# Laying SBUF out anew at fixed residues of 256 bytes in a hybrid decoder block (pooling mixer, gated linear attention, SwiGLU)

## The chip, the core and the metric

The kernel runs on one core of one Trainium2 chip. What counts is the device time of one execution in microseconds (us). Three runs of the kernel before took 1494.24, 1494.49 and 1495.74 us; their median is 1494.49 us. Where a figure below belongs to the profiled execution, that is one further run, of 1494.63 us.

## The reference, cut to what matters

The input is a block of 256 tokens by 2048 channels in float32. It goes through one decoder layer:

```
h = rms_norm(x);  z = h @ w_in                     # 2048 x 11280, split into p, q, k, v, g_lr, r, gate_logits
y_a = pool_mixer(p) @ w_branch_a                   # trailing means over windows of 2, 4, 8, 16 tokens
o   = gated linear attention(q, k, v, log_sigmoid(g_lr @ w_gate_up + b_gate) / 16)
y_b = (rms_norm(o) * silu(r)) @ w_branch_b
mixed = (sigmoid(g0) * y_a + sigmoid(g1) * y_b) @ w_out
x = x + rms_norm(mixed)
h = rms_norm(x)
x = x + rms_norm((silu(h @ w_ffn_gate) * (h @ w_ffn_up)) @ w_ffn_down)   # d_ff 5632
```

Nearly all the arithmetic is in the products with the weight matrices, 285 MB of float32 that come from HBM once.

## The kernel before, in words

**Precision.** TensorE multiplies float32r, a shortened float32. So each weight and each activation is split into a high part (a copy rounded to float32r) and a low part (the rest), and each product of the reference is three products on TensorE: weight high times activation high, weight low times activation high, weight high times activation low. These are the three `pe.matmul` lines that stand in a row everywhere: L337 to L339, L348 to L350, L408 to L410.

**Jobs and units.** The function `plan` lists jobs; a job makes 512 output columns for all 256 tokens (two row tiles `t`). A job is made of units, and each unit has one slot of split weights, `wh` and `wl`:

- A `Step` takes 256 rows of the weight matrix (two k-tiles): one DMA into `raw`, ScalarE copies it to `wh` (L317), VectorE subtracts to `wl` (L321). With weights as the moving operand it is twelve matmuls of 512 columns (L348 to L350), called wide below. Where the job is `across` (kinds p, q, k), the activations are the moving operand and the weights the stationary one: twenty-four matmuls of 256 columns (L337 to L339).
- A `Part` belongs to the 46 fast jobs. These do the first eight of their k-tiles by Strassen's scheme with seven products instead of eight, on two tiles of `blocks`: twelve matmuls of 256 columns each (L408 to L410), called narrow below. The seven are q1, q2 and q4, which use activations as they are, and r5, q6, q7 and r3, which use sums of activations (the list `COMBOS`). These sums have tiles of their own, made by `combine` and placed by `extra`: `x`, `ox` or `fx`.

A fast job with 16 k-tiles has four wide units and runs its units in the order of `merged`: q2, wide, q4, the next job's q1, r3, the next job's r5, wide, the next job's q6, wide, the next job's q7, wide. Jobs that follow each other keep this going without a gap.

**What sets the order.** The order is a list that the kernel builds at the start (`units`, `order`), walked by the loop at its end. `prepare_to` runs `BUFS` = 4 units ahead of the multiplications. SyncE's queue starts the weight DMAs, ScalarE and VectorE split, TensorE multiplies, and GpSimd starts a few accumulating DMAs and does small powers.

**Memory.** A tile pool places its tiles one behind the other, so where a tile starts depends on the sizes of what stands ahead of it. Weight slots come from pool `wp`, and a slot is as large as the widest unit needs, 4224 bytes per partition (16.5 times 256). Activations come from `one`: class `Act` makes, for each group of four k-tiles, a tile for the high parts and a tile for the low parts, 4096 bytes each. All of it stays in place, and tiles with the same tag share a place in turn.

**Starting residues.** A matmul reads two operands: the moving one streams through the array, the stationary one (128 columns of four bytes, 512 bytes per partition) is loaded ahead of it. What matters below is where an operand starts, modulo 256 bytes. In the built program of the kernel before these are:

| operand | before | after |
|---|---|---|
| weight slots `wh`, `wl` | 96 and 224, by turns | 64 |
| activations h (first norm), m, f, high and low | 0 | 0 |
| activations y, o, h2: groups 0 and 1 | 32 | 0 |
| activations o, h2: groups 2 and 3 | 160 | 0 |
| sums `x` | 160 | 128 |
| sums `ox` | 32 and 160 | 0 |
| sums `fx` | 224 | 128 |
| `blocks`, scratch | 224 | 64 |

Here y is the pooled branch, o the attention output, m the mixed branches, f the FFN's inner activations, h2 the second normed input.

Of the kernel before, what the change touches and what calls it, by code (L numbers as in the profile page):

```python
# [8 lines left out]
F32 = mybir.dt.float32  # L9
# [5 lines left out]
P = 128  # L15
# [17 lines left out]
BLOCKS = 3  # L33
AHEAD = 12
# [66 lines left out]
def tile_hybrid_block(ctx: ExitStack, tc: tile.TileContext, *aps):  # L101
# [6 lines left out]
    one = ctx.enter_context(tc.tile_pool(name="one", bufs=1))  # L108
    wp = ctx.enter_context(tc.tile_pool(name="wp", bufs=BUFS))
    scr = ctx.enter_context(tc.tile_pool(name="scr", bufs=SCRS))  # L110
    st = ctx.enter_context(tc.tile_pool(name="st", bufs=4))
# [6 lines left out]
    late = {}  # L118

# [18 lines left out]

    xa = [one.tile([P, D], F32, tag=f"X{t}", name=f"x{t}") for t in range(NT)]
    ident = one.tile([P, P], F32, tag="ident", name="ident")  # L140
    masks = two_st.tile([P, 64 * MASKED + P], I32, tag="masks", name="masks")
    counts = two_st.tile([P, 16], F32, tag="counts", name="counts")
    rows = [one.tile([n, P], F32, tag=f"rows{n}", name=f"rows{n}") for n in (16, 68)]
# [11 lines left out]
    first = st.tile([P, 4], F32, tag="first", name="first")  # L155
# [26 lines left out]
    def rstd_of(ss, n, width, tag):  # L182
        m = st.tile([P, width], F32, tag="ms", name=nm("ms"))
        dve.tensor_scalar(m, ss, 1.0 / n, EPS, op0=ALU.mult, op1=ALU.add)
        r = one.tile([P, width], F32, tag=tag, name=nm(tag))
        pool.tensor_tensor(r, m, mhalf[:, :width], op=ALU.pow)
        return r

    def extra(a):


        if a.name == "o":
            k = [two_st.tile([P, 2, 4, P], F32R, tag=f"K{i}", name=nm("ox")) for i in range(2)]
            q = [[two_st.tile([P, 4, P], F32R, tag=f"{x}{i}", name=nm("ox")) for i in range(2)] for x in ("Q", "AD")]
            return [tuple(x) for x in q] + [(x[:, 0], x[:, 1]) for x in k]
        if a.name[0] == "f":
            if not late:
                early.close()
                late["pool"] = ctx.enter_context(tc.tile_pool(name="late", bufs=1, reuse_waits="tile"))
            x = [late["pool"].tile([P, len(COMBOS), 4, P], F32R, tag=f"fx{i}", name=nm("fx")) for i in range(2)]  # L200
        else:
            x = [one.tile([P, len(COMBOS), 4, P], F32R, tag=f"R{i}", name=nm("x")) for i in range(2)]
        return [(x[0][:, n], x[1][:, n]) for n in range(len(COMBOS))]

    class Act:


        def __init__(self, name, groups, tag):
            self.name = name
            self.hi = [one.tile([P, 4, T], F32R, tag=f"{tag}{g}h", name=f"{name}{g}h") for g in range(groups)]  # L210
            self.lo = [one.tile([P, 4, T], F32R, tag=f"{tag}{g}l", name=f"{name}{g}l") for g in range(groups)]
# [85 lines left out]
    class Step:  # L297
# [16 lines left out]
        def high(self):  # L314
            self.load()
            self.hi = wp.tile([P, GK, self.j.width], F32R, tag="wh", name=nm("wh"))
            act.activation(self.hi, self.raw, AF.Copy)  # L317

        def low(self):
            self.lo = wp.tile([P, GK, self.j.width], F32R, tag="wl", name=nm("wl"))  # L320
            dve.tensor_tensor(self.lo, self.raw, f32(self.hi), op=ALU.subtract)  # L321
# [32 lines left out]
    class Part:  # L354
# [27 lines left out]
        def high(self):  # L382
            self.hi = wp.tile([P, 4, HW], F32R, tag="wh", name=nm("wh"))
            act.activation(self.hi, self.src, AF.Copy)  # L384

        def low(self):
            self.lo = wp.tile([P, 4, HW], F32R, tag="wl", name=nm("wl"))
            dve.tensor_tensor(self.lo, self.src, f32(self.hi), op=ALU.subtract)  # L388
# [69 lines left out]
    def total(part, ts, tag):  # L458

        w = len(ts)  # L460
        ss = st.tile([P, w], F32, tag="ss", name=nm("ss"))
        dve.tensor_reduce(ss, part[:, ts[0]:ts[0] + w, :], axis=mybir.AxisListType.X, op=ALU.add)
        return rstd_of(ss, D, w, tag)
# [71 lines left out]
    def r_done(n):  # L535
        def done(j, ts):
            glow = two_st.tile([P, NT, RANK], F32, tag="glow", name="glow") if n == 0 else None
# [29 lines left out]
    def gates_low(glow):  # L567
# [9 lines left out]
        gl["P"] = [one.tile([P, 4, T], F32, tag=f"B{2 + p}h", name=f"P{p}") for p in range(2)]  # L577
        gl["S"] = [one.tile([P, 4, T], F32, tag=f"B{2 + p}l", name=f"S{p}") for p in range(2)]
# [125 lines left out]
    def gla_out(h, t, v, silu):  # L704
# [7 lines left out]
        ss = st.tile([P, 1], F32, tag="sso", name=nm("sso"))  # L712
        act.activation(scratch(), ps, AF.Square, accum_out=ss)
        m = st.tile([P, 1], F32, tag="mso", name=nm("mso"))
        r = st.tile([P, 1], F32, tag="rso", name=nm("rso"))
# [23 lines left out]
    def chunk(tiles, t, n, tag, name):  # L739
        if not tiles:  # L740
            tiles += [one.tile([P, D], F32, tag=f"{tag}{a}", name=f"{name}{a}") for a in range(NT)]
        return tiles[t][:, n * CW:(n + 1) * CW]
# [68 lines left out]
    def out_done(n):  # L811
        def done(j, ts):
# [3 lines left out]
            for t in ts:  # L816
                if mg[t] is None:
                    mg[t] = one.tile([P, D], F32, tag=f"Y{t}", name=f"mg{t}")
# [66 lines left out]
    def down_done(part, n):  # L885
        def done(j, ts):
# [3 lines left out]
            for t in ts:  # L890
                if ff[t] is None:
                    ff[t] = one.tile([P, D], F32, tag=f"Y{t}", name=f"ff{t}")
# [8 lines left out]
            if part == 2 and n == 2:  # L901

                ss = st.tile([P, NT], F32, tag="ss", name=nm("ss"))
# [8 lines left out]
    def finish(t):  # L912
        m = st.tile([P, 1], F32, tag="ms", name=nm("ms"))
# [166 lines left out]
```

## Time and profile before

| quantity | value |
|---|---|
| median of three runs | 1494.49 us |
| the profiled execution | 1494.63 us |
| its span, first to last instruction | 1492.8 us |
| outside the span | 1.83 us |
| PE busy | 1475.1 us, 9156 matmuls |
| DVE busy | 1221.7 us |
| ACT busy | 907.7 us |
| POOL busy | 73.0 us |
| read from HBM | 284.84 MB, 194 GB/s over the span |

PE is TensorE's matrix side and PEld its loading of stationary operands, DVE is VectorE, ACT is ScalarE, POOL is GpSimd. L408 is line 408 of the kernel before. Matmuls overlap in the record: one of 256 columns is shown as 0.28 us long while the next one starts about 0.12 us after it. So what a matmul costs is read from the distance between starts, and the simplest way is to take a unit of twelve and read how long it is from its first start to the first start of what follows. A view by stretches does this: each row has the stretch, its length, the busy time of PE in it with the number of matmuls that touch it (a few more than start in it, because the neighbours overlap the edges), the granted clock and the load of the DMA engines.

### The profile page before, as it was taken

How to read it: one execution, taken by the hardware profiler on the slowest of the kernel's cores; microseconds unless marked ns; L12 is line 12 of the kernel's file. 1: busy time of each engine (PE TensorE's matmuls, PEld its weight loads, DVE VectorE, ACT ScalarE, POOL GpSimd, SP SyncE). 2: the span in 40 equal slices, each digit the busy share in tenths (PEclk: the TensorE clock that was granted, in tenths of full speed). 3: DMA queues.
4: the chain of work that ended last, by engine and by line, in shares of the span. 5: the costliest groups of instructions: out<-in, count | busy, mean ns of one | idle time of the engine just before them, and what ended most of it. 6: DMA issues, size and time to landing. Idle time of an engine off the chain costs nothing.

```text
span 1492.8 us, 23506 instructions
## 1 busy us (share of the span) xinstructions
PE 1475.1 (99%) x9156; PEld 1311.3 (88%) x9156; DVE 1221.7 (82%) x1359; ACT 907.7 (61%) x1185; POOL 73.0 (5%) x96
## 2 busy tenths in 40 slices
PE   8999999999999999999999999999999999999997
PEld 8988999888888888888878889898898888988886
DVE  6755445788899887799778899887889898888997
ACT  6457433556666665556566666666666665666663
POOL 2000000000100000000000000000000000000001
PEclk9999999999999999999999999999999999999999
DMA  8857665335668578659855677667766777676654
GB/s 286 272 173 226 215 192 176 124 111 175 228 206 248 190 241 268 201 155 295 247 173 168 215 220 231 214 220 228 236 212 213 225 226 218 224 235 222 204 180 141
DMA packets 88896, 314.70 MB, mean 211 GB/s; under 512 B 10140, under 2 KB 10352, under 8 KB 88528
## 3 DMA queue, kind: packets, MB, share of 16 engines
q1 hardware_dynamic: 77616, 279.15, 55.5%
q0 software_dynamic: 8160, 28.59, 10.0%
q10 hardware_dynamic: 3008, 5.45, 1.0%
q8 instruction: 72, 1.18, 0.3%
q14 instruction: 40, 0.33, 0.1%
HBM read 284.84 MB, written 4.19 MB: 194 GB/s over the span
## 4 chain that ended last, share of the span: by engine, by line
PE 88%; DVE 4%; issue 3%; DMA 2%; ACT 1%; POOL 0%; SPq 0%; DVEq 0%; ACTq 0%; POOLq 0%
PE acc L348 16%; PE acc L349 16%; PE acc L350 16%; PE ac L409 6%; PE ac L408 6%; PE ac L410 5%; PE acc L410 4%; PE acc L408 4%; PE acc L409 4%; PE acc L339 3%; PE acc L338 3%; PE acc L337 3%; PE tr L663 1%; DVE wl L321 1%; PE tr L180 1%
## 5 line engine op out<-in xcount | busy, mean ns | idle before, releaser
L317 ACT ACTIVATE wh<-raw 128x1024 fp32r<-128x1024 f32 (+1 forms) x336 | 355.3, 1059 | 316.9 <-PE acc L350 144.9
L321 DVE TENSOR_TENSOR wl<-raw,wh 128x1024 fp32r<-128x1024 f32 (+1 forms) x336 | 410.7, 1223 | 140.6 <-ACT wh L317 138.8
L388 DVE TENSOR_TENSOR wl<-blocks,wh 128x1024 fp32r<-128x1024 f32 x322 | 391.2, 1222 | 77.6 <-ACT wh L384 73.2
L384 ACT ACTIVATE wh<-blocks 128x1024 fp32r<-128x1024 f32 x322 | 338.1, 1058 | 157.0 <-PE acc L350 65.7
L408 PE MATMUL ac<-wh,x 128*128 128x256 f32 x396 | 111.1, 280 | 0.0
L410 PE MATMUL ac<-wh,x 128*128 128x256 f32 x396 | 110.9, 280 | 0.0
L409 PE MATMUL ac<-wl,x 128*128 128x256 f32 x396 | 110.9, 280 | 0.0
L380 POOL DMA_DIRECT2D blocks<-blocks x46 | 39.8, 865 | 822.0 <-DVE wl L321 365.9
L408 PEld LDWEIGHTS ac<-wh,x 128*128 128x128 f32 x396 | 74.4, 188 | 3.1
L409 PEld LDWEIGHTS ac<-wl,x 128*128 128x128 f32 x396 | 74.3, 188 | 2.9
L410 PEld LDWEIGHTS ac<-wh,x 128*128 128x128 f32 x396 | 74.8, 189 | 0.0
L348 PE MATMUL acc<-wh,h22h 128*128 128x512 f32 x176 | 70.1, 398 | 0.1
L349 PE MATMUL acc<-wl,h22h 128*128 128x512 f32 x176 | 69.4, 394 | 0.0
L350 PE MATMUL acc<-wh,h23l 128*128 128x512 f32 x176 | 69.3, 394 | 0.0
L348 PE MATMUL acc<-wh,h23h 128*128 128x512 f32 x176 | 69.2, 394 | 0.0
L350 PE MATMUL acc<-wh,h22l 128*128 128x512 f32 x176 | 69.2, 394 | 0.0
L349 PE MATMUL acc<-wl,h23h 128*128 128x512 f32 x176 | 69.2, 393 | 0.0
L373 DVE TENSOR_TENSOR blocks<-blocks,blocks 128x1024 f32<-128x1024 f32 x46 | 56.3, 1224 | 1.3
L369 DVE TENSOR_TENSOR blocks<-blocks,blocks 128x1024 f32<-128x1024 f32 x46 | 56.2, 1221 | 0.7
L371 DVE TENSOR_TENSOR blocks<-blocks 128x1024 f32<-128x1024 f32 x46 | 56.1, 1219 | 0.1
L348 PE MATMUL acc<-wh,h3h 128*128 128x512 f32 (+1 forms) x128 | 50.0, 391 | 0.0
L349 PE MATMUL acc<-wl,h3h 128*128 128x512 f32 (+1 forms) x128 | 49.9, 390 | 0.0
(538 smaller groups left out, 4112.7 us busy)
## 6 DMA issues: line engine op xcount, KB each, us to landing
raw<-in_w_in_dram SPq DMA_DIRECT2D x128, 512.0 KB, 4.1
raw<-in_w_ffn_gate_dram SPq DMA_DIRECT2D x48, 512.0 KB, 4.3
raw<-in_w_ffn_up_dram SPq DMA_DIRECT2D x48, 512.0 KB, 4.4
blocks<-blocks POOLq DMA_DIRECT2D x46, 512.0 KB, 6.1
blocks<-in_w_ffn_down_dram SPq DMA_DIRECT2D x44, 512.0 KB, 4.3
raw<-in_w_ffn_down_dram SPq DMA_DIRECT2D x44, 512.0 KB, 4.4
blocks<-in_w_in_dram SPq DMA_DIRECT2D x40, 512.0 KB, 4.4
blocks<-in_w_ffn_gate_dram SPq DMA_DIRECT2D x40, 512.0 KB, 4.3
```

The source lines that it names most:

```text
L317: act.activation(self.hi, self.raw, AF.Copy)
L321: dve.tensor_tensor(self.lo, self.raw, f32(self.hi), op=ALU.subtract)
L348: pe.matmul(ps, ah, hi[:, i, cs], start=first, stop=False, skip_group_check=j.fast)
L349: pe.matmul(ps, ah, lo[:, i, cs], start=False, stop=False, skip_group_check=j.fast)
L350: pe.matmul(ps, al, hi[:, i, cs], start=False, stop=last, skip_group_check=j.fast)
L369: dve.tensor_tensor(b12, b12, b22, op=ALU.add)
L373: dve.tensor_tensor(b21, b21, b12, op=ALU.add)
L384: act.activation(self.hi, self.src, AF.Copy)
L388: dve.tensor_tensor(self.lo, self.src, f32(self.hi), op=ALU.subtract)
L408: pe.matmul(dst, ah, wh, start=i == 0 and p in ("q1", "r5"), stop=False, skip_group_check=True)
L409: pe.matmul(dst, ah, wl, start=False, stop=False, skip_group_check=True)
L410: pe.matmul(dst, al, wh, start=False, stop=i == 3 and p in EARLY, skip_group_check=True)
```

## The change

Nothing of the arithmetic changes, and the order of instructions is the same on every engine. New pools stand at the start of SBUF: `his` for the high parts of activations, `los` for the low parts, `rest` for the tiles that hold Y and one of the two tiles of sums, and `st`, which moves up between them. Padding tiles of 64 and 192 bytes shift the pools `his` and `wp`. A helper `placed` takes a tile of a fixed size (4352 bytes for a weight slot, 17 times 256; 8448 bytes for a tile of sums, 33 times 256) and returns a view that starts some bytes into it. The residues that come out of it are the right column of the table above.

By the built programs, the distance D from the start of a matmul's moving operand to the start of the stationary operand that is loaded for the next matmul, modulo 256, changes as follows (counts of matmuls of 512 and of 256 columns; 192 matmuls of 264 columns and the small ones are left out, and a few single ones at other distances too):

| D | 0 | 32 | 64 | 96 | 128 | 160 | 192 | 224 |
|---|---|---|---|---|---|---|---|---|
| wide, before | 27 | 836 | 799 | 0 | 9 | 857 | 831 | 0 |
| wide, after | 14 | 0 | 125 | 0 | 0 | 0 | 3220 | 0 |
| narrow, before | 223 | 467 | 1177 | 571 | 305 | 437 | 1264 | 572 |
| narrow, after | 17 | 0 | 3158 | 0 | 6 | 0 | 1834 | 1 |

The narrow row holds the matmuls of 256 columns of the `across` jobs too (1152 of them; before, most of D = 96 and 224; after, D = 64). Beside this, small things move: the two staging tiles for the norm vectors (`rows`) are taken from the scratch buffers instead of places of their own, some small tiles in `st` get 2 buffers instead of 4 (`ms`, `sso`, `mso`, `rso`), `ss` and `first` go to `one`, and `glow` is allocated at the start. The built programs have the same waits on PE, DVE and SP apart from the first microseconds, where a few waits for scratch buffers on ACT fall on neighbouring instructions, and POOL has a wait on its own earlier work ahead of the powers for `rso`.

```
+LINE = 256
+PAD_A, PAD_B, PAD_W = 64, 0, 192
+ROOM_W = 4352
+AT_X, AT_F = 128, 64
+ROOM_X = 8448
...
     one = ctx.enter_context(tc.tile_pool(name="one", bufs=1))
+    his, st, los, rest = [ctx.enter_context(tc.tile_pool(name=n, bufs=b))
+                          for n, b in (("his", 1), ("st", 4), ("los", 1), ("rest", 1))]
     wp = ctx.enter_context(tc.tile_pool(name="wp", bufs=BUFS))
     scr = ctx.enter_context(tc.tile_pool(name="scr", bufs=SCRS))
-    st = ctx.enter_context(tc.tile_pool(name="st", bufs=4))
...
+    def placed(pool, shape, tag, name, lead=0, room=0):
+
+        n = 1
+        for k in shape:
+            n *= k
+        t = pool.tile([P, max(room // 4, n)], F32R, tag=tag, name=name)[:, lead // 4:lead // 4 + n]
+        if len(shape) == 2:
+            return t.rearrange("p (a b) -> p a b", a=shape[0])
+        return t.rearrange("p (a b c) -> p a b c", a=shape[0], b=shape[1])
...
+    for p_, n in ((his, PAD_A), (los, PAD_B), (wp, PAD_W)):
+        if n:
+            p_.tile([P, n // 4], F32, tag="pad", name=nm("pad"), bufs=1)
...
-    rows = [one.tile([n, P], F32, tag=f"rows{n}", name=f"rows{n}") for n in (16, 68)]
+    rows = [scratch()[:n, :P] for n in (16, 68)]
...
-        m = st.tile([P, width], F32, tag="ms", name=nm("ms"))
+        m = st.tile([P, width], F32, tag="ms", name=nm("ms"), bufs=2)
...
-            x = [late["pool"].tile([P, len(COMBOS), 4, P], F32R, tag=f"fx{i}", name=nm("fx")) for i in range(2)]
+            x = [placed(late["pool"], (len(COMBOS), 4, P), f"fx{i}", nm("fx"), AT_F, ROOM_X) for i in range(2)]
         else:
-            x = [one.tile([P, len(COMBOS), 4, P], F32R, tag=f"R{i}", name=nm("x")) for i in range(2)]
+            x = [placed(pool_, (len(COMBOS), 4, P), f"R{i}", nm("x"), AT_X, ROOM_X) for i, pool_ in enumerate((his, rest))]
...
-            self.hi = [one.tile([P, 4, T], F32R, tag=f"{tag}{g}h", name=f"{name}{g}h") for g in range(groups)]
-            self.lo = [one.tile([P, 4, T], F32R, tag=f"{tag}{g}l", name=f"{name}{g}l") for g in range(groups)]
+            self.hi = [placed(his, (4, T), f"{tag}{g}h", f"{name}{g}h") for g in range(groups)]
+            self.lo = [placed(los, (4, T), f"{tag}{g}l", f"{name}{g}l") for g in range(groups)]
...
-            self.hi = wp.tile([P, GK, self.j.width], F32R, tag="wh", name=nm("wh"))
+            self.hi = placed(wp, (GK, self.j.width), "wh", nm("wh"), room=ROOM_W)
...
-            self.lo = wp.tile([P, GK, self.j.width], F32R, tag="wl", name=nm("wl"))
+            self.lo = placed(wp, (GK, self.j.width), "wl", nm("wl"), room=ROOM_W)
...
-            self.hi = wp.tile([P, 4, HW], F32R, tag="wh", name=nm("wh"))
+            self.hi = placed(wp, (4, HW), "wh", nm("wh"), room=ROOM_W)
...
-            self.lo = wp.tile([P, 4, HW], F32R, tag="wl", name=nm("wl"))
+            self.lo = placed(wp, (4, HW), "wl", nm("wl"), room=ROOM_W)
...
-        ss = st.tile([P, 1], F32, tag="sso", name=nm("sso"))
+        ss = st.tile([P, 1], F32, tag="sso", name=nm("sso"), bufs=2)
...
-            tiles += [one.tile([P, D], F32, tag=f"{tag}{a}", name=f"{name}{a}") for a in range(NT)]
+            tiles += [(rest if tag == "Y" else one).tile([P, D], F32, tag=f"{tag}{a}", name=f"{name}{a}")
+                      for a in range(NT)]
```

More of the change, by code (lines that the diff above doesn't have):

```diff
@@ L141, in tile_hybrid_block @@
     masks = two_st.tile([P, 64 * MASKED + P], I32, tag="masks", name="masks")
+    glow = two_st.tile([P, NT, RANK], F32, tag="glow", name="glow")
     counts = two_st.tile([P, 16], F32, tag="counts", name="counts")
-    rows = [one.tile([n, P], F32, tag=f"rows{n}", name=f"rows{n}") for n in (16, 68)]
+    rows = [scratch()[:n, :P] for n in (16, 68)]
     cols = one.tile([P, 84], F32, tag="cols", name="cols")
@@ L153, in tile_hybrid_block @@
     pool.memset(mhalf, -0.5)
-    first = st.tile([P, 4], F32, tag="first", name="first")
+    first = one.tile([P, 4], F32, tag="first", name="first")
     act.activation(first, mhalf, AF.Copy)
@@ L460, in total @@
         w = len(ts)
-        ss = st.tile([P, w], F32, tag="ss", name=nm("ss"))
+        ss = one.tile([P, w], F32, tag="ss", name=nm("ss"), bufs=2)
         dve.tensor_reduce(ss, part[:, ts[0]:ts[0] + w, :], axis=mybir.AxisListType.X, op=ALU.add)
@@ L536, in done @@
         def done(j, ts):
-            glow = two_st.tile([P, NT, RANK], F32, tag="glow", name="glow") if n == 0 else None
             for t in range(NT):
@@ L576, in gates_low @@
         dve.tensor_tensor(gT[64:64 + RANK], g, f32(gT[:RANK]), op=ALU.subtract)
-        gl["P"] = [one.tile([P, 4, T], F32, tag=f"B{2 + p}h", name=f"P{p}") for p in range(2)]
-        gl["S"] = [one.tile([P, 4, T], F32, tag=f"B{2 + p}l", name=f"S{p}") for p in range(2)]
+        gl["P"] = [f32(placed(his, (4, T), f"B{2 + p}h", f"P{p}")) for p in range(2)]
+        gl["S"] = [f32(placed(los, (4, T), f"B{2 + p}l", f"S{p}")) for p in range(2)]
         for p in range(2):
@@ L711, in gla_out @@
             pe.matmul(ps, lo[:, s, :], v[:, tj, 0], start=False, stop=n == len(terms) - 1)
-        ss = st.tile([P, 1], F32, tag="sso", name=nm("sso"))
+        ss = st.tile([P, 1], F32, tag="sso", name=nm("sso"), bufs=2)
         act.activation(scratch(), ps, AF.Square, accum_out=ss)
-        m = st.tile([P, 1], F32, tag="mso", name=nm("mso"))
-        r = st.tile([P, 1], F32, tag="rso", name=nm("rso"))
+        m = st.tile([P, 1], F32, tag="mso", name=nm("mso"), bufs=2)
+        r = st.tile([P, 1], F32, tag="rso", name=nm("rso"), bufs=2)
         dve.tensor_scalar(m, ss, 1.0 / DV, EPS, op0=ALU.mult, op1=ALU.add)
@@ L817, in done @@
                 if mg[t] is None:
-                    mg[t] = one.tile([P, D], F32, tag=f"Y{t}", name=f"mg{t}")
+                    mg[t] = rest.tile([P, D], F32, tag=f"Y{t}", name=f"mg{t}")
                     xr[t] = one.tile([P, D], F32, tag=f"X{t}", name=f"xr{t}")
@@ L891, in done @@
                 if ff[t] is None:
-                    ff[t] = one.tile([P, D], F32, tag=f"Y{t}", name=f"ff{t}")
+                    ff[t] = rest.tile([P, D], F32, tag=f"Y{t}", name=f"ff{t}")
                 if part == 0:
@@ L901, in done @@
             if part == 2 and n == 2:
-                ss = st.tile([P, NT], F32, tag="ss", name=nm("ss"))
+                ss = one.tile([P, NT], F32, tag="ss", name=nm("ss"), bufs=2)
                 dve.tensor_reduce(ss, part3[:, :, :3], axis=mybir.AxisListType.X, op=ALU.add)
@@ L912, in finish @@
     def finish(t):
-        m = st.tile([P, 1], F32, tag="ms", name=nm("ms"))
+        m = st.tile([P, 1], F32, tag="ms", name=nm("ms"), bufs=2)
         dve.tensor_scalar(m, part3[:, t, 3:], 1.0 / D, rs["3"][:, t:t + 1], op0=ALU.mult, op1=ALU.add)
```

## The prediction

> **What bounds the kernel now.** I read the page first, then who TensorE waits for, then single stretches of TensorE's work. The page's head, its engines, the granted clock and the chain that ended last:
>
> ```profile
> span 1492.8 us, 23506 instructions
> PE 1475.1 (99%) x9156; PEld 1311.3 (88%) x9156; DVE 1221.7 (82%) x1359; ACT 907.7 (61%) x1185; POOL 73.0 (5%) x96
> PEclk9999999999999999999999999999999999999999
> PE 88%; DVE 4%; issue 3%; DMA 2%; ACT 1%; POOL 0%; SPq 0%; DVEq 0%; ACTq 0%; POOLq 0%
> ```
>
> TensorE (PE) is busy for 99% of the span at the full clock, and the chain runs through it. Its longest waits, in total, times and longest:
>
> ```profile
> PE tr L180 <- DMA x<-in_x_dram: 1.4, 3, 0.8
> PE tr L152 <- DVE scr L149: 1.1, 1, 1.1
> PE acc L337 <- ACT h3h L219: 1.0, 1, 1.0
> PE acc L349 <- DVE wl L321: 0.9, 2, 0.7
> ```
>
> The largest is 1.4 us, all for x at the start. So the kernel is as long as 3,360 wide and 5,016 narrow matmuls one behind the other (counted in the built program), and only what changes the distance from one start to the next can change the time. The change does not touch the number or order of matmuls. The question is whether that distance depends on where the operands lie. Stretches of TensorE, one unit each (columns: stretch, length, PE busy with the matmuls touched, clock, load of the DMA engines, GB/s); all are twelve matmuls from first start to first start, save rows three and four, which are twenty-four:
>
> ```profile
> 145.58:148.38 2.80, 2.80 (x13) 1.00 0.78 265
> 148.38:151.19 2.81, 2.81 (x14) 1.00 0.53 185
> 215.82:218.62 2.80, 2.80 (x27) 1.00 0.58 187
> 218.62:221.44 2.82, 2.82 (x27) 1.00 0.63 192
> 370.18:371.56 1.38, 1.38 (x13) 1.00 0.81 315
> 796.29:799.04 2.75, 2.75 (x13) 1.00 0.76 219
> 801.85:804.60 2.75, 2.75 (x14) 1.00 0.55 179
> 804.60:807.39 2.79, 2.79 (x14) 1.00 0.56 185
> 807.39:808.80 1.41, 1.41 (x13) 1.00 0.02 6
> 812.97:815.73 2.76, 2.76 (x15) 1.00 0.16 56
> 815.73:817.14 1.41, 1.41 (x14) 1.00 0.82 279
> 821.31:824.08 2.77, 2.77 (x14) 1.00 0.63 200
> 824.08:825.45 1.37, 1.37 (x14) 1.00 1.02 404
> 847.45:850.24 2.79, 2.79 (x14) 1.00 0.46 185
> 850.24:851.61 1.37, 1.37 (x14) 1.00 0.35 24
> 851.61:853.02 1.41, 1.41 (x14) 1.00 0.74 290
> 970.60:972.04 1.44, 1.44 (x14) 1.00 0.68 253
> 1404.96:1406.33 1.37, 1.37 (x14) 1.00 0.14 57
> ```
>
> In every row PE is busy throughout, so nothing was waited for, and the clock is 1.00. Yet equal work takes 2.75 to 2.81 us when wide and 1.37 to 1.44 us when narrow. The DMA load does not sort them: 1.37 us stands beside 1.02 and 0.14, 1.41 us beside 0.02 and 0.82. The distance D between a matmul's moving operand and the next matmul's stationary one does. It matters because both are read at once, as the loads show:
>
> ```profile
> 821.31 0.40 PE L348 MATMUL acc<-wh,h23h 128*128 128x512 f32 x1
> ...
> 821.32 0.19 PEld L349 LDWEIGHTS acc<-wl,h23h 128*128 128x128 f32 x1
> 821.55 0.19 PEld L350 LDWEIGHTS acc<-wh,h23l 128*128 128x128 f32 x1
> ```
>
> The load for L349 starts 0.01 us after the matmul of L348. With D from the built program, the wide rows are 2.80 us at D = 160 (145.58), 2.81 at 32 (148.38), 2.79 at 64 (804.60, 847.45) and 2.75 to 2.77 at 192 (796.29, 801.85, 812.97, 821.31). The narrow rows are 1.44 us at D = 0 (970.60). At D = 64 and 192 there are two lengths: at 64 1.38 (370.18), 1.37 (850.24, 1404.96) and 1.41 (815.73), at 192 1.37 (824.08) and 1.41 (807.39, 851.61). Which of the two comes depends on what ran before. Behind a wide unit of the same D it is the short one (824.08 behind 821.31 at 192; 850.24 behind 847.45 at 64). Behind a wide unit of the other D it is the long one (807.39 behind 804.60; 815.73 behind 812.97). 851.61, at 192 behind a narrow unit at 64, is long too. I take this to be two streams of reads that meet in the same part of SBUF and fall into a fixed rhythm.
>
> **The change part by part.** It removes and adds no work; each term is a number of units times a difference of two rows.
>
> Wide units. There are 3360/12 = 280. At D = 192 stand 831/12 = 69 now and 3220/12 = 268 after. The 199 that get there win 2.80 (the middle of 2.79 to 2.81) less 2.76 (the middle of 2.75 to 2.77), 0.04 us each: −8.0 us. Bounds: 0.02 us, from 2.79 and 2.77, gives −4.0; 0.06, from 2.81 and 2.75, gives −11.9.
>
> Narrow units without sums (q1, q2, q4, and the few that use `ox`): 1834/12 = 153, all at D = 192 after. By `merged`, q2 and q4 each stand right behind a wide unit at D = 192, which is the pattern of 824.08, so I take 1.37. q1 stands behind q4 with the same residues on both sides, so nothing changes between them, and I take 1.37 too; no row shows such a pair, since slots alternate today, and if q1 were at 1.41, 46 units would lose 0.04 us, 1.8 us. Before, 51 units last 1.385 us or less; the first of these is 370.18, the last 1404.96. So 102 more are short: 102 × (1.41 − 1.37) = −4.1 us.
>
> Narrow units with sums (r3, r5, q6, q7): 2015/12 = 168, at D = 64 after. q6 and q7 follow a wide unit at D = 192 (815.73: 1.41), r3 follows a narrow one at the other D (851.61: 1.41), r5 follows r3. I take 1.41 for all. All these 168 could also be short, −6.7 us; this goes into a rival.
>
> Narrow units at poor distances: 965 matmuls, 80 units, stand at D = 0, 128 or 160 now. Priced by 970.60 at D = 0, they go from 1.44 to 1.41 before anything else: 80 × 0.03 = −2.4 us. Those at 128 and 160 may be nearer 1.41, then it is −0.6 for D = 0 alone.
>
> `across` units: 1143 matmuls, 95 twelves. Now they take 2.80 and 2.82 us by turns for twenty-four, 1.405 for twelve. After, D = 64 throughout with 1.37 or 1.41 to choose from. No unit leads into it from a wide one of the same D, so I take 1.41: +0.5 us; the bounds are +0.5 and −3.3.
>
> The small edits cost nothing in my sum. Extra waits at the start fall on ACT, ahead of its weight copies; TensorE waits 1.4 us there for x itself, and a few tenths of ScalarE would hide behind that. POOL is busy 73.0 us of the span, and a wait of its powers on itself finds its own earlier work done. If that cover were gone, a weight copy at the start would come late; I allow 2 us for it, more than TensorE's longest wait there now.
>
> What is late next, when TensorE speeds up by a hundredth? VectorE, in the stages where it is busiest:
>
> ```profile
> 410.00:485.00 75.00, 75.00 (x446) 66.11 (x446) 70.06 (x82) 48.80 (x67) 5.77 (x7) 1.00 0.75 227
> 1100.00:1430.00 330.00, 329.82 (x2095) 296.38 (x2094) 297.06 (x303) 212.18 (x263) 12.82 (x15) 1.00 0.70 221
> ```
>
> The columns are PE, PEld, DVE, ACT, POOL. VectorE has 4.9 us of 75 and 33 of 330 free, so a hundredth (0.75 and 3.3 us) is still covered.
>
> Sum: −8.0 − 4.1 − 2.4 + 0.5 = −14.0 us. The profiled execution took 1494.63 us, of which 1492.8 is the span and 1.83 lies around it and stays. That run is 0.14 us above the median of 1494.49. So the forecast is 1494.5 − 14.0 = 1480.5 us.
>
> [...]
>
> **The rivals.** *All narrow units fall into the short rhythm.* Before, slots alternate by 128 bytes from unit to unit, and each change of residue can knock the rhythm over. After, nothing alternates, and a short rhythm could carry on through the sums and the `across` units. For it speaks that both distances allow 1.37; against it 815.73 and 851.61, where a change of D alone gave 1.41. Price: the remaining 418 − 153 = 265 narrow twelves win 0.04 us, 10.6 us: 1469.9 us.
>
> *Only the wide units gain.* q1, q2 and q4 go into the long rhythm, as 807.39 and 851.61 do at the same D. Then the 51 short units are lost: 51 × 0.04 = +2.0, and −8.0 − 2.4 + 0.5 + 2.0 = −7.9: 1486.6 us.
>
> *The distance does not carry over,* because the lengths come from something else that goes with it in this program, such as which tile or slot is used, and the new places bring the same mixture: 1494.5 us. For it speaks that the same D gives two lengths; against it, that four wide rows at 192 lie together below all others. [...]
>
> [...]
>
> **How the numbers follow.** Forecast 0.54, all short 0.17, wide only 0.13, no change 0.10, slower 0.06. A difference from no change can be told here from about 0.2%, 3.0 us. The first three are faster by more: 0.84. No change gives 0.09 within 0.2%; the slower case and a little of no change give 0.07. The range takes in wide-only and all-short with their bounds: 1466 (all-short with the wide units at 0.06: 1469.9 − 3.9) to 1493 (wide-only with 0.02 each and nothing else: 1490.5, and 2 us for the small edits). Outside lie slower, most of no change and the far ends of the others, some 0.2 in all.
>
> **What would show it.** Right: in the profile after, every wide unit takes 2.75 to 2.77 us; narrow units on h2, f, m at q1, q2, q4 take 1.37; units on `x` and `fx` take 1.41; TensorE stays 99% busy; TensorE's waits stay near a microsecond. All short: units on `fx` at 1.37 too. Wrong: wide units still at 2.80, or narrow ones at 1.44; or PE busy well under 99% with waits on VectorE's `wl`, which would mean that the gain was made and lost again.

## The result and the profile after

The changed kernel took 1477.76 us (median of four runs, 1477.51 to 1479.42). The kernel before, on the same chip, took 1495.12 us (1494.24 to 1496.41). The ratio is 0.9886, with a 95% interval of 0.9868 to 0.9903. The forecast was 1480.5 us. The profiled execution of the changed kernel took 1477.55 us.

The head of its page, the engines and the chain that ended last:

```profile
span 1475.7 us, 23511 instructions
PE 1454.2 (99%) x9156; PEld 1299.3 (88%) x9156; DVE 1219.9 (83%) x1359; ACT 907.6 (62%) x1185; POOL 73.0 (5%) x96
PE 85%; DVE 6%; issue 3%; DMA 3%; ACT 2%; POOL 0%; SPq 0%; DVEq 0%; ACTq 0%; POOLq 0%
```

The number of matmuls is the same, and PE's busy time fell by 20.9 us. The span fell by only 17.1 us. The rest shows in PE's waits (in total, times, longest):

```profile
PE tr L203 <- DMA x<-in_x_dram: 4.1, 6, 1.2
PE acc L372 <- DVE wl L344: 1.8, 2, 1.5
PE acc L371 <- ACT wh L340: 1.2, 3, 0.6
...
PE ac L432 <- DVE wl L411: 0.7, 2, 0.5
```

The waits for x at the start were 1.4 us before, those for `wl` of a wide unit 0.9. The waits for x differ between executions that have the same work at the start: 1.8 us in `e13_both` below, 3.4 in `e5_others`.

Now the same units as in the prediction, found by their place in the order of matmuls. Lines L360 to L362 are the `across` matmuls, L371 to L373 the wide ones and L431 to L433 the narrow ones. Columns: stretch, length, PE busy with the matmuls touched, clock, load of the DMA engines, GB/s.

```profile
143.92:146.67 2.75, 2.75 (x13) 1.00 0.73 253
146.67:149.42 2.75, 2.75 (x14) 1.00 0.49 146
214.19:217.02 2.83, 2.83 (x27) 1.00 0.55 185
217.02:219.84 2.82, 2.82 (x26) 1.00 0.61 184
367.81:369.23 1.42, 1.42 (x13) 1.00 0.73 291
796.88:799.63 2.75, 2.75 (x14) 1.00 0.53 159
799.63:801.04 1.41, 1.41 (x13) 1.00 0.15 61
807.96:809.38 1.42, 1.42 (x14) 1.00 0.84 317
816.31:817.72 1.41, 1.41 (x13) 1.00 0.98 398
842.54:843.90 1.36, 1.36 (x14) 1.00 0.34 24
843.90:845.26 1.36, 1.36 (x15) 1.00 0.75 292
961.34:962.72 1.38, 1.38 (x14) 1.00 0.81 327
1387.36:1388.71 1.35, 1.35 (x13) 1.00 0.54 218
```

The wide units that took 2.80, 2.81 and 2.79 us (145.58, 148.38 and 804.60 in the prediction's rows) take 2.75. The `across` units of 215.82 and 218.62 take 2.83 and 2.82, against 2.80 and 2.82 before. The narrow unit of 970.60 fell from 1.44 to 1.38, the one of 370.18 rose from 1.38 to 1.42. So narrow units still come in two lengths, and not as forecast: 816.31, at D = 192 behind a wide unit at 192, is long, and 961.34, one with sums at D = 64, is short.

From here on a narrow unit is called short at 1.35 to 1.38 us (113 to 115 ns a matmul) and long at 1.41 to 1.42 (118 ns). The spacings in ns are read from the start times in the trace, waits left out: a narrow unit counts by the median of its spacings, a wide one by the second half of its unit, where the spacing has settled. Where units are counted as standing behind one another, only those with no other matmul between them are taken, unless it is said otherwise; small matmuls, such as transposes, stand between some.

Two long stretches carry most comparisons below. The first holds 32 `across` units in a row, the second runs from the unit at 851.61 of the prediction to the one at 1404.96, 3,492 matmuls. Before:

```profile
159.60:249.54 89.94, 89.94 (x770) 1.00 0.64 200
851.61:1404.96 553.35, 553.35 (x3494) 1.00 0.71 223
```

After:

```profile
157.66:248.11 90.45, 90.45 (x769) 1.00 0.65 198
843.90:1387.36 543.46, 543.30 (x3495) 1.00 0.73 226
```

So 9.9 of the 17.1 us come from the second stretch, and the `across` stretch lost half a microsecond.

### The profile page after: what moved, and what is told of

It reads as the page before. It is cut to its first block, busy times and chain, and to the rows that moved or that the text cites. A ratio compares the mean times of both kernels' runs of the same rounds, so it can differ in the third digit from the quotient of the medians.

```text
span 1475.7 us, 23511 instructions
## 1 busy us (share of the span) xinstructions
PE 1454.2 (99%) x9156; PEld 1299.3 (88%) x9156; DVE 1219.9 (83%) x1359; ACT 907.6 (62%) x1185; POOL 73.0 (5%) x96
## 4 chain that ended last, share of the span: by engine, by line
PE 85%; DVE 6%; issue 3%; DMA 3%; ACT 2%; POOL 0%; SPq 0%; DVEq 0%; ACTq 0%; POOLq 0%
PE acc L372 15%; PE acc L373 15%; PE acc L371 15%; PE ac L432 5%; PE ac L431 5%; PE ac L433 5%; PE acc L433 4%; PE acc L432 4%; PE acc L431 4%; PE acc L362 3%; PE acc L360 3%; PE acc L361 3%; DVE wl L411 2%; DVE wl L344 2%; PE tr L685 1%
## 5 line engine op out<-in xcount | busy, mean ns | idle before, releaser
L431 PE MATMUL ac<-wh,x 128*128 128x256 f32 x396 | 110.4, 279 | 0.0
L433 PE MATMUL ac<-wh,x 128*128 128x256 f32 x396 | 109.8, 277 | 0.0
L431 PEld LDWEIGHTS ac<-wh,x 128*128 128x128 f32 x396 | 74.5, 188 | 2.9
L433 PEld LDWEIGHTS ac<-wh,x 128*128 128x128 f32 x396 | 74.4, 188 | 0.0
L372 PE MATMUL acc<-wl,h22h 128*128 128x512 f32 x176 | 69.6, 395 | 0.2
L371 PE MATMUL acc<-wh,h22h 128*128 128x512 f32 x176 | 69.4, 394 | 0.2 <-ACT wh L340 0.2
L373 PE MATMUL acc<-wh,h23l 128*128 128x512 f32 x176 | 69.3, 394 | 0.0
L373 PE MATMUL acc<-wh,h22l 128*128 128x512 f32 x176 | 69.2, 394 | 0.0
L372 PE MATMUL acc<-wl,h23h 128*128 128x512 f32 x176 | 69.1, 392 | 0.0
L371 PE MATMUL acc<-wh,h23h 128*128 128x512 f32 x176 | 68.4, 390 | 0.5 <-ACT wh L340 0.5
L371 PE MATMUL acc<-wh,h3h 128*128 128x512 f32 (+1 forms) x128 | 49.6, 387 | 0.0
L372 PE MATMUL acc<-wl,h3h 128*128 128x512 f32 (+1 forms) x128 | 49.5, 387 | 0.0
```

Of the source, the lines that this page charges most:

```text
L371: pe.matmul(ps, ah, hi[:, i, cs], start=first, stop=False, skip_group_check=j.fast)
L372: pe.matmul(ps, ah, lo[:, i, cs], start=False, stop=False, skip_group_check=j.fast)
L373: pe.matmul(ps, al, hi[:, i, cs], start=False, stop=last, skip_group_check=j.fast)
L431: pe.matmul(dst, ah, wh, start=i == 0 and p in ("q1", "r5"), stop=False, skip_group_check=True)
L433: pe.matmul(dst, al, wh, start=False, stop=i == 3 and p in EARLY, skip_group_check=True)
```

## The experiments

All started from the changed kernel, and all times stand beside runs of the kernel before on the same chip (medians 1494.86 to 1495.53). "Short" counts the narrow units of the fast jobs that fell into the short rhythm, of 322, in the profiled execution; the last two columns are the lengths of the two stretches.

| run | median us (range) | ratio (95%) | short | across stretch | long stretch |
|---|---|---|---|---|---|
| before | 1495.12 | | 55 | 89.94 | 553.35 |
| after | 1477.76 (1477.51–1479.42) | 0.9886 (0.9868–0.9903) | 241 | 90.45 | 543.46 |
| e1_shift32 | 1478.99 (1477.32–1479.21) | 0.9891 (0.9876–0.9906) | 248 | 90.46 | 542.83 |
| e2_one_pool | 1476.91 (1475.17–1478.46) | 0.9879 (0.9864–0.9894) | 239 | 90.45 | 543.67 |
| e3_alternate | 1484.46 (1483.63–1485.28) | 0.9928 (0.9911–0.9944) | 109 | 87.06 | 550.12 |
| e4_scan | 1495.51, one run | | 41 | 90.73 | 554.77 |
| e5_others | 1473.78 (1473.21–1474.70) | 0.9856 (0.9841–0.9871) | 270 | 87.07 | 543.37 |
| e6_same_d | 1484.63 (1480.83–1486.58) | 0.9925 (0.9905–0.9945) | 25 | 90.45 | 550.54 |
| e7_d0 | 1494.17 (1492.23–1495.40) | 0.9989 (0.9979–0.9999) | 2 | 92.15 | 554.82 |
| e8_step0 | 1481.83 (1480.39–1482.65) | 0.9906 (0.9889–0.9923) | 73 | 90.45 | 548.31 |
| e9_half_load | 1477.06, one run | | 223 | 90.45 | 543.39 |
| e11_scan_parts | 1485.91, one run | | 18 | 90.46 | 551.72 |
| e12_only_r | 1475.67 (1475.47–1477.18) | 0.9871 (0.9855–0.9888) | 243 | 90.45 | 543.59 |
| e13_both | 1471.35 (1468.36–1473.12) | 0.9843 (0.9830–0.9857) | 257 | 87.06 | 542.81 |

**e1_shift32** moves all weights, activations and sums by 32 bytes and leaves the distances D between them as they are. It tells the distance from the absolute start.

```
-PAD_A, PAD_B, PAD_W = 64, 0, 192
+PAD_A, PAD_B, PAD_W = 96, 0, 192
```

> Every operand of TensorE starts 32 bytes later than in the changed kernel (weights at 96, activations at 32, sums at 160), and scratch and blocks do too; all distances D stay as they are. Theory (the distance counts): the time of the changed kernel, 1477.8 us within 2, wide units 2.75 us, short narrow ones 1.36 to 1.37. Rival (what counts is that starts lie on multiples of 64 bytes): most of the 17.4 us is lost, 1488 us or more.

It took 1478.99 us, within the theory's bounds. A shift of all starts by 32 bytes makes no difference that the runs can tell (ratio 0.9891 against 0.9886).

**e2_one_pool** keeps all residues but puts high and low parts into one pool again.

```
-    his, st, los, rest = [ctx.enter_context(tc.tile_pool(name=n, bufs=b))
-                          for n, b in (("his", 1), ("st", 4), ("los", 1), ("rest", 1))]
+    his, st = [ctx.enter_context(tc.tile_pool(name=n, bufs=b)) for n, b in (("his", 1), ("st", 4))]
+    los = rest = his
```

> High parts, low parts, Y and the sums come from one pool in the order in which they are made; the residues stay those of the changed kernel. Theory (the distance modulo 256 counts): 1477.8 us within 2. Rival (the separate pools for high and low parts count): back towards the kernel before, 1490 us or more.

It took 1476.91 us, so the separate pools are worth nothing that the runs can tell (ratio 0.9879 against 0.9886). The residues carry the gain.

**e3_alternate** lets the weight slots start at 64 and 192 by turns again, as the kernel before did at 96 and 224.

```
-ROOM_W = 4352
+ROOM_W = 4224
```

> Weight slots are 4224 bytes again, so they start at 64 and 192 by turns; all else as in the changed kernel. Half of the wide units go from D = 192 to 64, and each unit changes the residue. Theory: 134 wide units at 2.80 instead of 2.75 us cost 6.7 us, and the rhythm of the narrow ones is knocked over between units, so that half of the roughly 220 short ones become long at 0.05 us each, 5.5 us more: 1490 us, 1486 to 1493. Rival (aligned starts or pools count, not the distance): 1477.8 us within 2.

At 1484.46 us it went the way that the theory said, but by 6.7 us instead of 12, less than its range allowed. The wide units split as expected (130 uninterrupted ones at D = 64 with 233 ns, 126 at 192 with 229), and the narrow ones lost their short rhythm (109 short). What was not foreseen is the `across` stretch, which fell from 90.45 to 87.06 us and took 3.4 us off the loss.

**e4_scan** moves the weights by another multiple of 16 bytes in each job, to see many distances in one run.

```
+    def lead_of(j):
+        return 0 if j.width > CW else 16 * (jobs.index(j) % 16)
...
-            self.hi = placed(wp, (GK, self.j.width), "wh", nm("wh"), room=ROOM_W)
+            self.hi = placed(wp, (GK, self.j.width), "wh", nm("wh"), lead=lead_of(self.j), room=ROOM_W)
```

The same lead goes to the other three tiles of weights.

> One look. The weight slots' start is moved by 16 bytes per job, through 16 steps and round again, so that each distance D in steps of 16 stands in one run; slots as large as in the changed kernel, work unchanged. Theory: the length of a steady wide unit depends on D alone: 2.75 us at D = 192, 2.80 at 64, 2.80 at 32 and 2.80 to 2.82 at 160, as in the kernel before; D = 0 and 128 at 2.80 or worse; narrow 1.44 at 0. Time between 1490 and 1505 us. Rival (the residues are not what counts): all steps alike, 2.75 and 1.37 to 1.41, 1478 us.

Five wide units of this run, at D = 64, 16, 0, 192 and 64 by the built program:

```profile
567.92:570.72 2.80, 2.80 (x14) 1.00 0.96 252
629.22:632.06 2.84, 2.84 (x13) 1.00 0.90 309
634.90:637.63 2.73, 2.73 (x14) 1.00 1.03 269
734.94:737.68 2.74, 2.74 (x14) 1.00 0.98 375
920.41:923.20 2.79, 2.79 (x14) 1.00 1.04 157
```

All five are twelve matmuls of 512 columns, and they go from 2.73 to 2.84 us by where their operands lie. By distance the mean spacing was 228.6 ns at D = 0, 228.9 at 192, 230.6 at 208, 231 to 232 at 80, 144, 176 and 240, 233 at 32, 64, 112, 128, 160 and 224, 234 to 235 at 48 and 96, and 235.6 at 16. The total, 1495.51 us, is where the theory put it. One expectation missed: D = 0, poor for narrow units as expected (119.6 ns), is the best for wide ones. Narrow units were short only at four distances: 64 (17 of 25), 144 (10 of 14), 192 (10 of 24) and 240 (4 of 21).

**e5_others** moves what the other engines write while TensorE reads.

```
-AT_X, AT_F = 128, 64
+AT_X, AT_F = 128, 192
...
-    for p_, n in ((his, PAD_A), (los, PAD_B), (wp, PAD_W)):
+    for p_, n in ((his, PAD_A), (los, PAD_B), (wp, PAD_W), (scr, 128)):
```

> Only the places of what the other engines use move: scratch buffers and blocks start at 192 instead of 64 (modulo 256). Every operand of TensorE keeps its residue, except the few sums ox, which go to 128: some 100 narrow matmuls, 8 units, change from D = 192 to 64. Theory (the distances of TensorE's own two operands decide): within 2 us of the kernel after on this chip, 1475.8 to 1479.8. Rival (a good part of the 17 us comes from where scratch and blocks lie, which ScalarE, VectorE and GpSimd write while TensorE reads): 5 us or more slower than the kernel after, 1483 or above.

It took 1473.78 us: faster than the kernel after, which neither side had. The intervals of the two ratios still touch, but the trace shows the gain. The long stretch is as in the kernel after (543.37 us); the `across` stretch shows where the gain is, with one of its units (the one that takes 2.82 us after, at 217.02):

```profile
160.79:247.86 87.07, 87.07 (x769) 1.00 0.66 206
217.94:220.66 2.72, 2.72 (x26) 1.00 0.57 203
```

These units have D = 64 in both kernels and are long in the one, short in the other. My premise that all operands of TensorE stay put had a hole: small matmuls read from scratch too, among them the pooling's (L548, the stationary operand) and the gate's (L606, the moving operand `gT`). The pooling's do not explain the gain: the `across` units right behind them are long in both kernels (118 ns a matmul in the kernel after). The gate's are the last small matmuls ahead of the `across` stretch, with 18 wide units at D = 192 between. Through all 18 the spacings are 226, 229 and 232 ns by turns, but in the kernel after the 226 stands behind L373 and in this run behind L371. So I take the rhythm in which the stretch starts to have been set there; no run changed these operands alone. The theory had a hole as well: the distance alone does not tell which of the two lengths a unit takes. That led to the next question, what hands a rhythm on.

**e6_same_d** gives all wide and narrow units the one distance 192.

```
-AT_X, AT_F = 128, 64
+AT_X, AT_F = 0, 192
```

> Sums start at 0 instead of 128, so that all wide units and all narrow ones have D = 192, and only the across units (D = 64) differ. Theory (a short rhythm carries on from unit to unit as long as it is not knocked over, and it decides, not the value 64 or 192 as such): the narrow units with sums stay at 1.36 us as they are at D = 64, the ones without sums go from two thirds short to nearly all, about 40 units times 0.06 us: 1475.5, between 1473 and 1478. Rival (each change from a wide unit to a narrow one at D = 192 falls into either rhythm by chance, two thirds short): 168 units with sums go from 145 short to 110 short, 35 times 0.06: 1480, between 1479 and 1482.

It took 1484.63 us, above both. Seven units of it in a row (wide; q4 and the next job's q1, without sums; r3 and r5, with sums; wide; q6, with sums), and the long stretch:

```profile
840.31:843.05 2.74, 2.74 (x14) 1.00 0.50 184
843.05:844.47 1.42, 1.42 (x14) 1.00 0.28 43
844.47:845.88 1.41, 1.41 (x14) 1.00 0.80 290
845.88:847.29 1.41, 1.41 (x14) 1.00 0.97 398
847.29:848.71 1.42, 1.42 (x15) 1.00 0.03 12
848.71:851.45 2.74, 2.74 (x14) 1.00 0.88 232
851.45:852.87 1.42, 1.42 (x14) 1.00 1.04 202
844.47:1395.01 550.54, 550.38 (x3495) 1.00 0.72 223
```

The first three units have every operand where the kernel after has it, yet the narrow ones are long here (1.42 and 1.41) and short there (842.54 and 843.90: 1.36). So the difference comes from before them. Counted over the whole run: behind a long narrow unit 112 of 112 narrow ones were long, and with a wide unit between 152 of 153. Almost nothing in this run brings the short rhythm back. In the kernel after, the step from q1 (D = 192) to r3 (D = 64) does: 8 of 14 such units behind a long one were short.

**e7_d0** has the same even layout, but at the distances 0 and 128.

```
-PAD_A, PAD_B, PAD_W = 64, 0, 192
+PAD_A, PAD_B, PAD_W = 64, 0, 128
...
-AT_X, AT_F = 128, 64
+AT_X, AT_F = 128, 128
```

> As fixed and as even as the kernel after, but weight slots start at 0: wide units and narrow ones without sums at D = 0, narrow ones with sums at 128, across at 0. Theory (the distance decides, and it goes by the one-unit figures of the run with scanned leads): 280 wide units gain about 0.005 us each, 1.4; some 250 narrow and across twelves at 0 go from about 1.38 to 1.435 us, +14; 168 with sums at 128 from 1.365 to 1.427, +10: 1500, between 1494 and 1504, so no better than the kernel before. Rival (any layout with nothing alternating falls into a good rhythm): 1480 or less.

It took 1494.17 us, at the lower edge of what the theory gave: 2 of 322 narrow units were short, both at D = 192, while the wide ones went to 227.6 ns and won more than I had set. An even layout is not enough: at D = 0 and 128 no unit fell into the short rhythm, while in the kernel after, at 64 and 192, 241 of 322 did.

**e8_step0** puts only the wide units at D = 0 and leaves the narrow ones at 64 and 192.

```
+    def lead_of(j):
+        return 0 if j.width > CW or j.across else 192
...
-            self.hi = placed(wp, (GK, self.j.width), "wh", nm("wh"), room=ROOM_W)
+            self.hi = placed(wp, (GK, self.j.width), "wh", nm("wh"), lead=lead_of(self.j), room=ROOM_W)
```

The low part in `Step` gets the same lead.

> Only the weights of the wide units that are not across start 192 bytes further on, at 0: wide units at D = 0, narrow units as in the kernel after (64 and 192). The run with scanned leads had single wide units at D = 0 of 226.7 to 231 ns per matmul, mean 228.6, against 229.2 on average in the kernel after. Theory (each unit's spacing follows from its own D, and a steady run at D = 0 reaches 226.7 ns): 3228 times 2.5 ns, 8 us less, 1470, if the narrow units keep their rhythm. If D = 0 gives the mean of the scan, 1476. Rival (the narrow units' short rhythm is handed on by a wide unit at D = 192): narrow units behind a wide one go long, up to 240 units times 0.055 us, +13 us: 1485 or more.

The same seven units as in e6_same_d:

```profile
840.89:843.65 2.76, 2.76 (x14) 1.00 0.50 199
843.65:845.07 1.42, 1.42 (x14) 1.00 0.31 35
845.07:846.48 1.41, 1.41 (x15) 1.00 0.77 288
846.48:847.84 1.36, 1.36 (x15) 1.00 1.01 413
847.84:849.20 1.36, 1.36 (x15) 1.00 0.06 24
849.20:851.95 2.75, 2.75 (x15) 1.00 0.82 228
851.95:853.37 1.42, 1.42 (x13) 1.00 1.07 208
```

One reads the rule off these rows. Long behind the wide unit (843.65), long next to it at the same distance (845.07), short from the step to D = 64 on (846.48, 847.84), and long again behind the next wide unit at D = 0 (851.95). Counted, 33 of 36 narrow units came out long behind a wide one that stood behind a short one. In the kernel after, with the wide units at 192, it was none of 132. Where small matmuls stood between, 10 of 13 came out long. The time, 1481.83 us, lies between theory and rival: the wide units won (227.4 ns on average), and the loss of rhythm (73 short) cost more.

**e12_only_r** tests this rule: as e6_same_d, but the sums r5 and r3 back at 128, so that each job has one step from 192 to 64, and q6 and q7 stay at 192.

```
+    def spots(pool, tag, name, at):
+        t = pool.tile([P, ROOM_X // 4], F32R, tag=tag, name=name)
+        at = [at, at + 4096 + 128, at + 6144 + 128, at + 2048]
+        return [t[:, o // 4:o // 4 + 512].rearrange("p (a b) -> p a b", a=4) for o in at]
```

> The kernel with all sums at 0 (1484.6 us), but the two sums r5 and r3 back at 128: r3 and r5 have D = 64 again, q6 and q7 stay at 192 like q1, q2 and q4. Theory, formed from the last batch: a rhythm is handed on from unit to unit, also through a wide unit at 192; nothing at one and the same distance brings back the short one, and the step from q1 (192) to r3 (64) is what does. So one repair in each job is enough: of 321 narrow units some 230 or more are short, against 25 with all at 192, 205 times 0.055 us = 11 us: 1473.5, between 1471 and 1478. Rival (D = 64 is the better distance as such, and 192 falls long by itself): only the 87 units of r3 and r5 win 0.055 us each, 4.8: 1480, between 1478.5 and 1482.

It took 1475.67 us with 243 short units, as the theory said. The rival's 1480 is out. Four units of it, those of 843.05 to 848.71 in e6_same_d, and the long stretch:

```profile
840.37:841.73 1.36, 1.36 (x13) 1.00 0.29 27
841.73:843.09 1.36, 1.36 (x14) 1.00 0.76 244
843.09:844.45 1.36, 1.36 (x14) 1.00 1.01 413
844.45:845.81 1.36, 1.36 (x14) 1.00 0.22 87
841.73:1385.32 543.59, 543.38 (x3495) 1.00 0.73 226
```

The first two, q4 and q1, have the operands and the D = 192 that they have in e6_same_d. Placing the sums of r3 and r5, which they do not use, 128 bytes further on brought them from 1.42 and 1.41 to 1.36. Against the kernel after, the long stretch is the same (543.46 us there) and the intervals of the two ratios overlap, so e12_only_r undoes the loss of e6_same_d and shows no further gain.

**e9_half_load** asks what makes the spacing: it halves the load of one stationary operand in three, and leaves out half of the rows of that product.

```
-                        pe.matmul(ps, ah, lo[:, i, cs], start=False, stop=False, skip_group_check=j.fast)
+                        pe.matmul(ps[:64], ah[:, :64], lo[:, i, cs], start=False, stop=False, skip_group_check=True)
```

> The layout of the kernel after, but the second of the three wide matmuls (line 372) uses only 64 of the 128 stationary columns, so its load reads half as many bytes while the matmul of line 371 streams. Half of the rows of that product are left out. Theory (the moving operand and the load of the next stationary operand get in each other's way in SBUF): the spacing behind line 371 falls from 229 ns by several ns, towards half of what the meeting costs; the matmuls of lines 372 and 373, followed by full loads, stay at 229 or within 2 ns. Rival (the load costs nothing, and 229 ns is what 512 columns take by themselves): all three stay at 229 ns, and the total at 1477.8. Mean over the three gives the total: 2 ns off one in three is 2.2 us.

The loads by themselves (columns: shape and count, then busy time in us and mean ns of one, then idle time before them in us), a full one and a halved one:

```profile
L373 PEld LDWEIGHTS acc<-wh,h23l 128*128 128x128 f32 x176 | 33.1, 188 | 16.1
...
L372 PEld LDWEIGHTS acc<-wl,h23h 128*64 128x64 f32 x176 | 23.6, 134 | 5.7
```

The load went from 188 to 134 ns, and the spacing behind L371, while it runs, from 227.4 to 227.5 ns (means over all wide matmuls outside of waits; behind L372 it is 229.8 in both, behind L373 230.8 and 229.7). On the load the rival holds: 54 ns less of it beside the matmul left the spacing where it was.

**e11_scan_parts** scans the narrow units' distance behind wide units at D = 0.

```
-            self.hi = placed(wp, (4, HW), "wh", nm("wh"), room=ROOM_W)
+            self.hi = placed(wp, (4, HW), "wh", nm("wh"), lead=16 * (jobs.index(self.j) % 16), room=ROOM_W)
```

The low part likewise; the rest as e8_step0.

> Wide units at D = 0 throughout (227 ns a matmul), and the weights of the narrow units start 16 bytes further on from job to job, to find a distance at which the narrow units are short (113 ns) behind a wide unit at D = 0. With both at 64 and 192 they were short in 73 of 321. Theory by the earlier scan: none of the narrow distances except 64, 144, 192 and 240 is ever short; 144 is the one that could be short by itself; the others 117 to 120 ns. The total would be near 1492, between 1487 and 1497. Rival (a wide unit at D = 0 breaks every short rhythm): 144 is long as well.

The total of 1485.91 us was below my range. On the question itself the rival holds: at D = 144 one unit of 14 was short, against 10 of 14 with the wide units at 144 too. Of the other distances 64 had 12 of 25, 192 had 3 of 24 and 240 had 2 of 21.

**e13_both** joins e12_only_r and e5_others.

```
-    for p_, n in ((his, PAD_A), (los, PAD_B), (wp, PAD_W)):
+    for p_, n in ((his, PAD_A), (los, PAD_B), (wp, PAD_W), (scr, 128)):
```

The tiles of sums are placed so that they keep the residues of e12_only_r.

> The two layouts that beat the kernel after, put together: q6 and q7 back at 192 with r3 and r5 at 64 (1475.7 by itself), and scratch buffers and blocks at 192 instead of 64 (1473.8 by itself). Theory: the two gains lie in different units. The first is in the narrow units of the fast jobs; the second is in the across units, 42 of 48 short instead of 8, about 34 units of twenty-four times 4.4 ns, 3.6 us. So they add: 1475.7 less 3.6, 1472, between 1470 and 1474. Rival (both only hold the rhythm that the chip happens to fall into, and are not two separate gains): 1474 to 1477, no better than the better of the two.

It took 1471.35 us, the fastest of all: 24.1 us below the kernel before (1495.47 on that chip). Its engines, its `across` stretch and its long stretch:

```profile
PE 1449.2 (99%) x9156; PEld 1294.7 (88%) x9156; DVE 1219.7 (83%) x1359; ACT 907.3 (62%) x1185; POOL 73.1 (5%) x96
156.12:243.18 87.06, 87.06 (x769) 1.00 0.67 206
836.21:1379.02 542.81, 542.73 (x3495) 1.00 0.73 227
```

The time is where the theory put it, and the rival's 1474 is out. The `across` stretch gives 3.4 us against e12_only_r (forecast: 3.6). The rest is less clear: the long stretch is only 0.65 us below the kernel after, and the interval overlaps that of e5_others, so how much q6 and q7 at 192 add is not settled. That it beats the kernel after is: 0.9830 to 0.9857 against 0.9868 to 0.9903.

## Why the prediction was right, and which term was mis-sized

**The bound.** Right. PE stays at 99% of the span, and but for the waits named below the change follows from the spacing of matmuls.

**Wide units, −8.0 us.** Right, a little small. Summing the distances from each matmul's start to the next, the wide ones outside of waits give −9.7 us. The spacing settled at 229 ns in 240 of the 256 units that nothing interrupts. The 16 others, 233 ns, all stood right behind a long narrow unit at D = 64.

**Narrow units without sums, −4.1 us plus their part of the poor distances.** The size came out (−4.2 us) by luck, the pattern did not: I took all of them as short, and 96 of 146 were. Of the 138 on h, o, m, f and h2, 64 went from long to short and 5 the other way, where I had counted on 102; but each of the 64 gained 0.06 us rather than 0.04, 3.9 us together, 23 of them 0.07 because they left D = 160 as well.

**Narrow units with sums, nothing beyond their part of −2.4 us.** This is the term that was mis-sized. I took them long, because 815.73 and 851.61 were long behind a change of D. In fact 145 of 176 were short (I had counted 168 units), and they gave −6.7 us. The rows of before misled me, since its weight slots alternate. There, and in `e3_alternate`, the narrow unit right behind a wide one at 192 goes by the change of D, as I had read it: at D = 64 it was long 18 times of 18 (34 of 34 in `e3_alternate`), at D = 192 short 13 times of 13 (41 of 42). With the slots at one residue this no longer holds: in the kernel after 72 of 86 such units at D = 64 were short, 69 of them behind a narrow one that was short. One row of the prediction itself spoke against the reading: 370.18 is short at D = 64, and the wide unit ahead of it stands at D = 32. The rival "all short" had the right idea (nothing alternates, so a rhythm carries on), but it would have had the rest short too, and 81 of 322 stayed long.

**`across`, +0.5 us.** Right for the stretch: 40 of all 48 units were long, and the `across` stretch grew by 0.5 us. Summed over all 48, outside of waits, it was −0.2, a small term of the other sign.

**Small edits and waits, nothing.** Not quite: the intervals with a wait in them grew by 3.7 us in all. I had allowed 2 us, and took them as covered. So −9.7 − 4.2 − 6.7 − 0.2 + 3.7 is −17.1 us of span, against −14.0 forecast; the terms together gave 6.8 us more than forecast, most of it in the sums and the wide units, and 3.7 of that were given back in waits. Of these 2.7 are waits for x, which differ between executions.

**The other rivals.** That the distance doesn't carry over is out by the result itself. Were the layout worth nothing, e1 to e8 would all have taken the same time; they lie between 1473.78 and 1495.51 us. The slower case, which had 0.06, is out as well: the ratio is 0.9886. That starts on multiples of 64 bytes are what counts is out by e1_shift32: 32 bytes off, the time is the same.

**What stays open.** I took the spacing for two streams of reads that meet in the same part of SBUF; no run shows that. Shown is that the spacings go with the distance modulo 256 between a matmul's moving and the next one's stationary operand (wide units from 228.6 ns at D = 0 to 235.6 at 16 in `e4_scan`; 241 narrow units of 322 short at 64 and 192 in the kernel after, none at 0 and 128 in `e7_d0`), and with what ran before (112 of 112 in `e6_same_d`). That it is the next one's operand shows at the end of a wide unit in the kernel after: where the 226 ns stand behind L371, the last spacing is 233.3 ns if the next unit's operand makes its D 64, and 231.6 if it stays 192 (69 and 67 units). Not shown is by what mechanism: in `e9_half_load` a load of 134 ns instead of 188 moved the spacing behind L371 by 0.1 ns, which speaks against a cost that goes by the amount read. Nor did a run test by itself which operand of the small matmuls puts the `across` units into the short rhythm when scratch lies at 192.

## What to carry to other kernels

When TensorE is busy all the time, as here for 99% of the span, measure the spacing of equal matmuls one by one. In the kernel before, at a granted clock of 1.00, wide units took 2.75 to 2.81 us and narrow ones 1.37 to 1.44 for the same work, by where their operands lay and what ran before, and a fixed placement modulo 256 bytes, at the distances 64 and 192, was worth 1% (ratio 0.9886) without changing the work. Do not stop at the best distance of each unit by itself: e8_step0 gave the wide units a better one and lost 4 us, because the narrow units behind them fell out of their rhythm. Waits move the result too: in the profiled execution they took back 3.7 of 20.8 us. But they differ from run to run: in `e13_both`, where PE is busy 5 us less, PE is idle for 17.3 us of the span, in the kernel after for 21.5, in the kernel before for 17.7.

## What the runs showed of the hardware that was not expected

- Matmuls of 256 columns had two steady spacings at D = 64 and 192, in the kernel after 113 or 114 ns (241 units) and 118 or 119 (81), also at the same operands (q4 and q1, 1.42 and 1.41 us in `e6_same_d`, 1.36 in `e12_only_r`). They keep the one that they are in: in `e6_same_d`, 112 of 112 narrow units directly behind a long one at the same distance were long.
- A wide unit at D = 192 hands the rhythm on: in `e6_same_d` 152 of 153 narrow units behind such a wide unit were long where the narrow one before it was long, and in `e12_only_r` 131 of 134 were short where that one was short. Small matmuls between go with a loss of the short rhythm: 77 of 98 such units came out long behind a short one over the eight runs named below, against 11 of 972 with nothing between. A wide unit at D = 0 (227 ns) ends the short rhythm (33 of 36 in `e8_step0`).
- The mean spacing of a wide unit does not tell which rhythm it carries (229 ns behind short units, and behind long ones at D = 192; 233 in 16 of 23 behind long ones at D = 64 in the kernel after), but the order of its spacings does. They are 226, 229 and 232 ns by turns. Over the eight runs with wide units at D = 192 (after, e1, e2, e5, e6, e9, e12, e13), the narrow unit behind was short 986 times of 988 where the 226 stood behind the first of the three matmuls (L371), and long 345 times of 356 where it did not.
- With the weight slots at one residue, a step of D from 192 to 64 between two adjacent narrow units turns a long rhythm into a short one in about two of three cases (8 of 14 in the kernel after, 6 of 15 in `e12_only_r`, 35 of 44 in `e8_step0`; 108 of 155 over the kernel after, e1, e2, e5, e8, e9, e12 and e13). With alternating slots it did so in 19 of 38 (`e3_alternate`) and 1 of 19 (the kernel before).
- The best distance depended on the width: at D = 0 matmuls of 512 columns had their shortest spacing (means 228.6 ns in `e4_scan`, 227.6 in `e7_d0`, 227.4 in `e8_step0`; 226.7 in the shortest unit of `e4_scan`) and matmuls of 256 columns a long one (119.6 ns in `e4_scan`, 1.44 us for twelve, 120 ns, at 970.60 of the kernel before).
